# A hybrid encoder trunk: recurrence products issued in turns between halves of the array, and a bias for the decay's constant

## The chip, the cores and the metric

The kernel runs on one core of one Trainium2 chip. The metric is the device time of one execution in microseconds (us). Before the change three runs took 1224.38, 1223.29 and 1211.89 us; their median is 1223.29.

## What is computed

Two layers act on 256 tokens of 1024 channels, all in float32. Layer 0 mixes tokens with a bidirectional RWKV-7 recurrence, layer 1 with dilated attention. Behind each stands a mixture of 32 experts, of which every token uses two. Each part works on a normalised and modulated stream and adds to it; a last norm closes the trunk. The change lies in layer 0's mixer alone:

```python
def lora(xin, A, Bm, act):
    return jnp.einsum('zbsr,zre->zbse', act(jnp.einsum('bsd,zdr->zbsr', xin, A)), Bm)

w_log = -jax.nn.softplus(-(w0[:, None, None, :] + lora(xw, w1, w2, jnp.tanh))) - 0.5
decay = jnp.exp(-jnp.exp(w_log))
a = jax.nn.sigmoid(a0[:, None, None, :] + lora(xa, a1, a2, lambda t: t))
# per head of 64 channels and per direction z, step by step:
sa = jnp.einsum('bhvk,bhk->bhv', state, a_t)
state = state * w_t[:, :, None, :] + sa[..., None] * b_t[:, :, None, :] + v_t[..., None] * k_t[:, :, None, :]
y_t = jnp.einsum('bhvk,bhk->bhv', state, r_t)
```

## The kernel before, in words

The recurrence (`rwkv`) works on eight pairs of heads; a pair is 128 channels, so one head stands on partitions 0 to 63 and the other on 64 to 127. The 256 tokens are four chunks of 64. Both directions z run at once: at step s one is at chunk s, the other at chunk 3 - s. For each pair i:

- `project(i)` makes keys and receptances (`kr`), the decay's logarithm (`L`), the learning rate (`at`) and the values (`v`). `L` and `at` are second halves of LoRAs of rank 64 per direction. `L` has a 65th row: the hidden layer `hidw` ends in a row of ones and the weights in `w0`, so that the product adds it. `at` is added as a bias on ACT.
- `ready(i)` is `scale_keys(i)` and `chunks(i)`. `chunks` makes the chunk products `G`: for each direction and each head four products of 64 rows of the array by 128 columns into one PSUM bank, which DVE reads twice under masks (GV and GI).
- `inverse(i)` inverts the chunks' matrices by half-precision products (`iv`).
- `recur(i)` has for each of four steps: `R` (state times keys, not at step 0), `U` (inverse times R), `S` (the new states: an identity product carries the old one, two products add to it; not at step 3) and `Y` (the output: one product with the state, not at step 0, and two with `U`). `R` and `U` are issued in turns between the halves of the array already.
- `finish(i)` has the head norm, the bonus and the gate.

`weave` emits `recur(i)`, `inverse(i + 1)`, `finish(i - 1)`, `ready(i + 2)` and `project(i + 3)` side by side under priorities; a scheduler then sets the order of each engine's instructions. Every engine runs its own in that order, so an instruction that waits holds up all behind it. PSUM has eight banks: `pp` three (projections), `ps` two (`G`, `rn`, `sT`, `BT`, `R2`), `iv` two, `ch` one (`recur`).

A ring of 1 MB buffers takes the weights in the order of their use, and the queue SP issues each transfer when a buffer is free. The ring is two buffers long at first and grows as parts of the recurrence's memory are given back (`later`, behind pairs 4 to 7 and at the end). Line 266 is the helper of all matmuls, so they are told apart by their tiles. A float32 matmul appears in the trace as two passes.

Of the kernel before, what the change touches and what calls it, by code (L numbers as in the profile page):

```python
# [10 lines left out]
F32 = mybir.dt.float32  # L11
# [4 lines left out]
ALU = mybir.AluOpType  # L16
# [15 lines left out]
# share of the tensor engine's work of the streams that are woven, and their offset in priority  # L32
# [3 lines left out]
# eighths of the modulations that go with each pair of heads, and with each projection of the attention  # L36
ADA_PAIRS, ADA_PARTS = (0, 6, 6, 6, 8, 8, 8, 6, 0, 0, 0), (4, 4, 4, 4, 4, 4, 4, 4, 0)

# [1 line left out]
C_TMG, C_CMG, C_ADAB, C_C, C_FG = 0, 16, 32, 128, 136  # L40
N_COLS = 144
# (from here on for the recurrence only)
C_MU, C_KK, C_KA, C_RK, C_LNW, C_LNB, C_A0 = (N_COLS + n for n in (0, 48, 56, 64, 72, 80, 88))

# [1 line left out]
def _constants():  # L46
# [8 lines left out]
    # from here on for the recurrence only  # L55
# [34 lines left out]
def _half_constants():  # L90
    """identity, its negative, a 64 x 64 identity, the masks of the inverse's levels"""
    a, b = np.arange(64)[:, None], np.arange(64)[None, :]
    lv = np.zeros((64, 6, 64))
    for l in range(6):
        s = 1 << l
        lv[:, l] = ((a // (2 * s)) == (b // (2 * s))) & ((a // s) != (b // s))
    lv -= np.eye(64)[:, None]
    lv = lv.reshape(64, -1)
    e = np.tile(np.eye(64), (2, 1))
    return np.concatenate([np.eye(128), -np.eye(128), e, np.concatenate([lv, lv], 0),  # L100
                           np.kron(np.eye(2), lv[:, 0:64])], 1).astype(np.float16)
# [6 lines left out]
def _attn_constants():  # L108
    """Negative distances under the masks of the three groups; the tokens in the order even, odd."""
# [10 lines left out]
class Stream:  # L120
    """Blocks of weights, in the order in which they are used, through a ring of tiles.

    While a phase leaves room, a second pool lengthens the ring for the blocks before `limit`."""
# [38 lines left out]
    def spare(self):  # L162
        """A tile of the ring, once it holds all the blocks that are left."""
# [8 lines left out]
    def take(self, *names):  # L172
        """The next blocks; those taken before are used up."""
# [8 lines left out]
    def done(self):  # L182
        """The blocks taken last are used up."""
        for j in self.held:
            self.tiles.pop(j)
            self.owner.pop(j)[2] -= 1
        self.held = []
        self.fill()


# modulations (layer, kind, eighth) that are worked out before and during each token mixer
# [45 lines left out]
def trunk(ctx, tc, names, aps, out, stages=("rwkv", "moe0", "attn", "moe1"), dbg=None, ring=2):  # L237
# [16 lines left out]
    def banks(**n):  # L254
        """The banks of PSUM of a phase, by their uses."""
# [16 lines left out]
    def weave(*streams):  # L272
        """Emits streams side by side, each in step with its share of the tensor engine's work."""
# [87 lines left out]
    def ada_first(tag, acc):  # L361
        """Shift and scale of the first norm, by both engines."""
# [23 lines left out]
    def ada(i, m, k, tag="ps"):  # L386
        """An eighth of one of the six modulations."""
# [31 lines left out]
    def split(hi, lo, src, by, eng=None):  # L419
        """src times `by` (a power of two) as the sum of two numbers in half precision"""  # L420
# [12 lines left out]
    def scales(i, which):  # L433
        """columns of the modulated norm: scale, shift"""
# [8 lines left out]
    def new_sums(n=2):  # L443
        """the sums of squares of the tokens, in n parts of the channels"""
# [13 lines left out]
    def normalised(xn, tags):  # L458
        """the normalised stream in [d, t], two eighths of the channels in a bank each"""
# [17 lines left out]
    def transposed(j, behind=False):  # L477
        """a quarter of the stream's channels in [d, t]"""
# [9 lines left out]
    class Router:  # L488
        """Logits of the router, as the parts of x come in: its scale per token is put to the products."""
# [5 lines left out]
        def start(self):  # L495
            """The scaled weights, the part of the shift."""
# [14 lines left out]
        def hold(self, tag):  # L511
            """The bank and the sums that the parts of x go to."""
# [3 lines left out]
        def feed(self, t, c, junk):  # L516
            """a tile of tokens, half of the channels"""
# [23 lines left out]
    def gated(w, gate, k):  # L541
        """the rows of an output projection (k blocks side by side), times the gates of its columns"""
# [8 lines left out]
    def add_out(ps, t, c, by=1.0):  # L551
        """x += ps * by, in half of the channels of a tile of tokens"""
# [5 lines left out]
    def ada_share(n, tag="ps"):  # L558
        """The next n eighths of the modulations that go with layer 0."""
# [5 lines left out]
    def rwkv(pool):  # L565
        ctx2.enter_context(banks(pp=3, ps=2, iv=2, ch=1))
        cst_rw.append(pool.tile([128, 104], F32, name="colr"))
        nc.gpsimd.dma_start(out=cst_rw[0], in_=ap["p_colr"])
        sub = tc.alloc_tile_pool(name="sub", bufs=2, side="right", reuse_waits="tile")
        # (what the even pairs of heads use is given back before what the odd ones use)  # L570
# [5 lines left out]
        def pieces(tag):  # L576
            """tiles that are used before the recurrence needs their places"""
# [29 lines left out]
        # sigmoid(z) = 1/2 + tanh(z/2)/2, so that 1 + (a - 1) k_a = tanh k_a/2 + (1 - k_a/2)  # L607
        ka0, ka1 = (pool.tile([128, KD], F32, name=n) for n in ("ka0", "ka1"))
        a0h = pool.tile([128, 2 * KD], F32, name="a0h")
        # h, and half of both neighbours less h  # L610
# [3 lines left out]
        # (past the ends lies a zero, which the shift does not move)  # L614
# [32 lines left out]
        hidw = [sup.tile([65, S], F32, name=f"hidw{z}", bufs=1) for z in range(2)]  # L647
        hida = sup.tile([128, S], F32, name="hida", bufs=1)
        hidg = even.tile([128, 2, S], F32, name="hidg")

        def hidden():
            """LoRA hidden layers, [rank, t]"""
# [5 lines left out]
            for z in range(2):  # L658
                P.memset(hidw[z][64:65, :], 1.0)
                A.activation(out=hidw[z][0:64, :], in_=ps[64 * z:64 * z + 64, 0:S], func=AF.Tanh)  # L660
# [28 lines left out]
        # (two matrices of 64 x 64 each, on the diagonal)  # L689
# [18 lines left out]
        def both(t):  # L708
            """for both directions"""
            return t.unsqueeze(1).to_broadcast([128, 2] + list(t.shape[1:]))  # L710

        def project(i):
            """Projections of heads 2i and 2i + 1."""
# [9 lines left out]
            # 1 / max(|k k_k|, 1e-12) of each head, [t, (half of t, head)]  # L723
# [10 lines left out]
            w2 = vl[0:65, 1024:1280].rearrange("p (z n) -> p z n", z=2)  # L734
            a2 = vl[:, 1280:1408]
            ps = bank(name="L", tag="pp")
            L = sup.tile([128, 2, S], F32, name="L")
            for z in range(2):
                mm(ps[:, z * S:(z + 1) * S], w2[:, z, :], hidw[z])
            Lf = L.rearrange("p z t -> p (z t)")  # L740
            A.activation(out=Lf, in_=ps, func=AF.Tanh, scale=0.5)
            V.tensor_scalar(out=Lf, in0=Lf, scalar1=0.5 * DEC, scalar2=0.5 * DEC, op0=ALU.mult, op1=ALU.add)
            yield
            at = sup.tile([128, 2, S], F32, name="at")
            for z in range(2):
                ps = bank(name="at", tag="pp")
                mm(ps[:, 0:S], a2[half(z), :], hida[half(z), :])
                A.activation(out=at[:, z], in_=ps[:, 0:S], func=AF.Tanh,
                             scale=0.5, bias=a0h[:, 8 * z + i:8 * z + i + 1])
            w = ws[i] = dict(rn=rn, L=L, at=at, kT=krT[:, 0], rT=krT[:, 1])  # L750
            # values: channel-major, and token-major and centred by head
# [16 lines left out]
        def head_bcast(ps, v, n):  # L768
            """ps[channel, t] = v[t, head of the channel], for n blocks of 128 tokens"""
# [5 lines left out]
        def scale_keys(i, w):  # L775
            """Removal key, decays and the scaled operands, in [d, t]."""
            L, at, kT, rT = w["L"], w["at"], w["kT"], w["rT"]
            # sums of the logarithms over each chunk, in the directions' orders
# [4 lines left out]
            # running decays of each chunk, with a one before the first step: e1 up to a step, e3 up to the one before  # L783
# [30 lines left out]
            # bonus: (sum over the head) * v  # L814
# [4 lines left out]
            # (in use for three turns)  # L819
# [4 lines left out]
        def place(z, hh, c):  # L824
            """of a chunk's inverse: half of the partitions, number"""
            return half(1 - c % 2), (z * 2 + hh) * 2 + c // 2

        def chunks(i, w):
            """Chunk products, masked; token-major copies; the value part of the right-hand sides."""
# [4 lines left out]
            for z in range(2):  # L834
                for hh in range(2):
                    ps = bank(name="G")
                    for c in range(4):
                        mm(ps[:, c * 128:(c + 1) * 128], BK[half(hh), z, c, :], AR[half(hh), z, c, :])
                    for o, t in ((0, GV), (64, GI)):
# [5 lines left out]
            # the strictly triangular parts in two half-precision parts: half q holds chunk parity 1 - q  # L845
# [19 lines left out]
            # token rows of the recurrence: chunk parity p has its values on half p  # L865
# [16 lines left out]
        def inverse(i, w):  # L882
            """The chunks' (1 - A)^-1, transposed. By halves of ever larger blocks, in half precision; the residual
            is then taken with all of A's digits, and two terms of its series make up for it."""
# [15 lines left out]
            def parts(t):  # L900
                """The two blocks of the diagonal."""
                return [t[half(q), :, 64 * q:64 * q + 64] for q in range(2)]

            def spread(t, ps):
                """onto the diagonal, from PSUM"""
# [8 lines left out]
            # (Ah is A - 1 in half precision: A T - T has a diagonal of -1 and the blocks of A T below it)  # L914
# [48 lines left out]
        def recur(i, w):  # L963
            """The recurrence over chunks, both directions at once."""
# [3 lines left out]
            for s in range(4):  # L968
# [21 lines left out]
                if s < 3:  # L990
                    pS = bank(name="S", tag="ch")
                    for hh in range(2):
                        h, n = half(hh), slice(64 * hh, 64 * hh + 64)
# [958 lines left out]
```

## Time and profile before

| | before |
|---|---|
| median of three runs | 1223.29 us |
| the runs | 1224.38, 1223.29, 1211.89 us |
| span of the profiled execution (it has no other time) | 1225.3 us |
| PE busy | 1086.9 us (89%) |
| DVE busy | 660.5 us (54%) |
| ACT busy | 449.9 us (37%) |
| mean granted clock of TensorE | 0.936 |
| bytes moved | 322.46 MB, mean 263 GB/s |

Time is read from the stretch in which something happens, not from the shares over the whole span: the recurrence is the first 490 us or so, then come the experts of layer 0, the attention and the experts of layer 1. Matmuls are pipelined, so a group's cost is best read from its start to the start of the next group on PE, or over its first start to its last end.

### The profile page before, as it was taken

What the parts mean: (1) busy time and instruction counts of PE and PEld (TensorE: products, weight loads), DVE (VectorE), ACT (ScalarE), POOL (GpSimd) and SP (SyncE); (2) the same over time, 40 slices, a digit from 0 to 9 for tenths busy, and PEclk for the clock granted to TensorE, in tenths of its full rate; (3) what the DMA queues carried; (4) which work ended last, traced back from release to release, by engine and by line L of the source; (5) the groups of instructions that cost most, each with busy time, mean ns of one, the idle gap of its engine ahead of it and who ended that gap; (6) DMA issues with size and microseconds to landing.
All of it is one profiled execution on the core that took longest, in us unless ns stands there. A gap on an engine that the chain in (4) does not pass through costs nothing. (4 is left out here: it accounts for less than half of the span.)

```text
span 1225.3 us, 22879 instructions
## 1 busy us (share of the span) xinstructions
PE 1086.9 (89%) x9460; PEld 725.7 (59%) x9460; DVE 660.5 (54%) x1453; ACT 449.9 (37%) x940; POOL 177.8 (15%) x128
## 2 busy tenths in 40 slices
PE   4679999999999899897988879899988998799886
PEld 4556777777777664543443258778877864354432
DVE  8875477787774733522121166989986563122112
ACT  3326454464562552210010066546544531011002
POOL 6600001001120610000000012212283200000000
PEclk8789999999995999898998989989998999999989
DMA  9253164344352055898999996887653498989995
GB/s 373 101 206 117 35 204 125 123 156 133 106 173 103 2 241 221 333 422 352 422 421 421 420 419 240 315 319 290 237 197 138 168 361 358 417 366 421 421 420 229
DMA packets 53188, 322.46 MB, mean 263 GB/s; under 512 B 5922, under 2 KB 6562, under 8 KB 21458
## 3 DMA queue, kind: packets, MB, share of 16 engines
q1 hardware_dynamic: 51986, 316.49, 66.3%
q0 software_dynamic: 512, 2.30, 0.5%
q10 hardware_dynamic: 576, 2.10, 0.5%
q8 instruction: 78, 1.28, 0.4%
q14 instruction: 36, 0.29, 0.1%
HBM read 319.82 MB, written 1.05 MB: 262 GB/s over the span
## 5 line engine op out<-in xcount | busy, mean ns | idle before, releaser
L266 PE MATMUL gu<-wring,xT 128*32 128x512 f32 x1024 | 132.5, 619 | 16.9 <-DMA wring<-in_w_moe_dram 9.9
L358 DVE SCALAR_TENSOR_TENSOR acc<-aring,silu,acc 128x512 f32<-128x512 f32 x140 | 114.4, 849 | 9.5 <-DMA aring<-in_w_ada_dram 9.3
L425 POOL TENSOR_TENSOR wl<-wring,wh 128x1024 f16<-128x1024 f32 x24 | 57.2, 2383 | 407.1 <-DMA wring<-in_w_qkv_dram 241.0
L266 PE MATMUL qkv<-hl,wh 128*128 128x256 f16 x384 | 106.3, 277 | 2.0 <-DVE hl L1614 2.0
L266 PE MATMUL qkv<-hh,wl 128*128 128x256 f16 x384 | 106.4, 278 | 1.8 <-DVE wl L431 1.8
L266 PE MATMUL qkv<-hh,wh 128*128 128x256 f16 x384 | 106.6, 278 | 1.6 <-ACT hh L1613 1.6
L266 PEld LDWEIGHTS gu<-wring,xT 128*32 128x32 f32 x1024 | 31.8, 112 | 99.9 <-issue 80.4
L266 PEld LDWEIGHTS <-wh 128*128 128x128 f16 x768 | 76.4, 100 | 13.1 <-issue 3.6
L431 DVE SCALAR_TENSOR_TENSOR wl<-wring,wh 128x1024 f16<-128x1024 f32 x56 | 74.0, 1327 | 16.4 <-ACT wh L427 16.3
L266 PE MATMUL dn<-wring,hidT 128*32 128x256 f32 x1024 | 66.3, 407 | 18.1 <-ACT hidT L1416 18.0
L266 PE MATMUL acc<-y,back 128*128 128x512 f32 (+1 forms) x144 | 66.0, 581 | 10.3 <-DVE y L1443 8.1
L427 ACT ACTIVATE wh<-wring 128x1024 f16<-128x1024 f32 x56 | 58.6, 1050 | 35.4 <-PE qkv L266 30.8
L266 PEld LDWEIGHTS xT<-oh,x 128*128 128x128 f32 x512 | 59.0, 192 | 21.1 <-issue 9.2
L1218 DVE SCALAR_TENSOR_TENSOR sg<-sg,gu 128x256 f32<-128x256 f32 x16 | 6.7, 420 | 119.1 <-ACT sg L1217 119.1
L1443 DVE TENSOR_TENSOR y<-dn,ga 128x512 f32<-128x512 f32 x28 | 19.4, 692 | 88.9 <-PE dn L266 57.4
L266 PE MATMUL xT<-oh,x 128*128 128x128 f32 x512 | 63.5, 280 | 2.5 <-DVE oh L1327 2.5
L1217 ACT ACTIVATE sg<-gu 128x256 f32<-128x256 f32 x16 | 6.1, 383 | 153.1 <-PE gu L266 153.1
L266 PEld LDWEIGHTS dn<-wring,hidT 128*32 128x32 f32 x1024 | 32.1, 116 | 48.5 <-ACT hidT L1416 21.9
L1359 ACT ACTIVATE back<-bT 128x256 f32<-128x256 f32 x16 | 6.1, 384 | 131.7 <-PE acc L266 131.7
L266 PE MATMUL qkv<-wl,hh 128*128 128x256 f16 x192 | 54.0, 281 | 0.4 <-POOL wl L425 0.4
L266 PE MATMUL qkv<-wh,hl 128*128 128x256 f16 x192 | 53.9, 281 | 0.0
L266 PE MATMUL qkv<-wh,hh 128*128 128x256 f16 x192 | 53.9, 281 | 0.0
(341 smaller groups left out, 2292.0 us busy)
## 6 DMA issues: line engine op xcount, KB each, us to landing
wring<-in_w_moe_dram SPq DMA_DIRECT2D x192, 1024.0 KB, 19.8
aring<-in_w_ada_dram SPq DMA_DIRECT2D x96, 512.0 KB, 4.0
wring<-in_w_qkv_dram SPq DMA_DIRECT2D x36, 1024.0 KB, 8.5
wring<-in_w_kr_dram SPq DMA_DIRECT2D x8, 1024.0 KB, 5.1
wring<-in_w_vl_dram SPq DMA_DIRECT2D x8, 704.0 KB, 4.1
wring<-in_w_rwo_dram SPq DMA_DIRECT2D x4, 1024.0 KB, 5.9
wring<-in_w_ato_dram SPq DMA_DIRECT2D x4, 1024.0 KB, 6.5
ga<-in_p_adab_dram ACTq DMA_DIRECT2D x4, 512.0 KB, 3.8
```

The source lines that it names most:

```text
L266: return nc.tensor.matmul(out=o, lhsT=lhsT, rhs=rhs, start=start, stop=stop, **kw)
L358: V.scalar_tensor_tensor(out=acc[:, s], in0=w[:, s], scalar=silu[:, k:k + 1], in1=acc[:, s], op0=ALU.mult, op1=ALU.add)
L425: eng.tensor_tensor(out=lo, in0=src, in1=hi, op=ALU.subtract)
L427: A.activation(out=hi, in_=src, func=AF.Copy, scale=by)
L431: V.scalar_tensor_tensor(out=lo, in0=src, scalar=by, in1=hi, op0=ALU.mult, op1=ALU.subtract)
L1217: A.activation(out=o, in_=ps[:, 0:256], func=AF.Tanh, scale=0.5)
L1218: V.scalar_tensor_tensor(out=o, in0=o, scalar=1.0, in1=ps[:, 0:256], op0=ALU.add, op1=ALU.mult)
L1359: A.activation(out=back, in_=ps[:, 0:S], func=AF.Copy)
L1443: V.tensor_tensor(out=y, in0=py[c], in1=gates[i, 5][:, c * 512:(c + 1) * 512], op=ALU.mult)
```

## The change

In `chunks`, `G` opens two banks, one for each head, and issues the four chunks' products in turns between the heads, that is between the upper and the lower rows of the array. In `recur`, `S` issues the two identity products first, one for each half of rows and columns, and then the others in turns between the column halves; `Y` issues the two products with the state first and then the others in turns. The decay's LoRA loses its 65th row: `hidw` is one tile of 128 rows (rank 64 for both directions), the weights stand in 128 columns like those of `at`, `L` and `at` of one direction share a bank, and `w0` is added as a bias of the tanh (`w0h`, half of it, made once on DVE).

```diff
-        a0h = pool.tile([128, 2 * KD], F32, name="a0h")
+        a0h, w0h = (pool.tile([128, 2 * KD], F32, name=n) for n in ("a0h", "w0h"))
...
+        V.tensor_scalar(out=w0h, in0=col(C_W0, 2 * KD), scalar1=0.5, scalar2=None, op0=ALU.mult)
-        hidw = [sup.tile([65, S], F32, name=f"hidw{z}", bufs=1) for z in range(2)]
-        hida = sup.tile([128, S], F32, name="hida", bufs=1)
+        hidw, hida = (sup.tile([128, S], F32, name=n, bufs=1) for n in ("hidw", "hida"))
...
-            for z in range(2):
-                P.memset(hidw[z][64:65, :], 1.0)
-                A.activation(out=hidw[z][0:64, :], in_=ps[64 * z:64 * z + 64, 0:S], func=AF.Tanh)
+            A.activation(out=hidw, in_=ps[:, 0:S], func=AF.Tanh)
...
-            for z in range(2):
-                mm(ps[:, z * S:(z + 1) * S], w2[:, z, :], hidw[z])
+            pair = [bank(name="L", tag="pp") for _ in range(2)]
+            for n, hid in enumerate((hidw, hida)):
+                for z, ps in enumerate(pair):
+                    mm(ps[:, n * S:(n + 1) * S], vl[half(z), 1024 + 128 * n:1152 + 128 * n], hid[half(z), :])
+            for n, (t, b) in enumerate(((L, w0h), (at, a0h))):
+                for z, ps in enumerate(pair):
+                    A.activation(out=t[:, z], in_=ps[:, n * S:(n + 1) * S], func=AF.Tanh,
+                                 scale=0.5, bias=b[:, 8 * z + i:8 * z + i + 1])
             Lf = L.rearrange("p z t -> p (z t)")
-            A.activation(out=Lf, in_=ps, func=AF.Tanh, scale=0.5)
...
-            at = sup.tile([128, 2, S], F32, name="at")
-            for z in range(2):
-                ps = bank(name="at", tag="pp")
-                mm(ps[:, 0:S], a2[half(z), :], hida[half(z), :])
-                A.activation(out=at[:, z], in_=ps[:, 0:S], func=AF.Tanh,
-                             scale=0.5, bias=a0h[:, 8 * z + i:8 * z + i + 1])
...
             for z in range(2):
-                for hh in range(2):
-                    ps = bank(name="G")
-                    for c in range(4):
+                pair = [bank(name="G") for _ in range(2)]
+                for c in range(4):
+                    for hh, ps in enumerate(pair):
                         mm(ps[:, c * 128:(c + 1) * 128], BK[half(hh), z, c, :], AR[half(hh), z, c, :])
+                for hh, ps in enumerate(pair):
                     for o, t in ((0, GV), (64, GI)):
...
-                    for hh in range(2):
-                        h, n = half(hh), slice(64 * hh, 64 * hh + 64)
-                        if s > 0:
+                    hs = [(half(hh), slice(64 * hh, 64 * hh + 64)) for hh in range(2)]
+                    if s > 0:
+                        for h, n in hs:
                             mm(pS[h, 0:128], IDENT[h, n], ST[h, :, n], start=True, stop=False, skip_group_check=True)
-                        for z in range(2):
-                            c = cz[z]
+                    for z, c in enumerate(cz):
+                        for h, n in hs:
                             mm(pS[h, z * 64:z * 64 + 64], BT[:, c % 2, z, c // 2, n], UV[:, z, c, n],
...
-                for z in range(2):
-                    h = half(cz[z] % 2)
-                    if s > 0:
+                hs = [half(c % 2) for c in cz]
+                if s > 0:
+                    for z, h in enumerate(hs):
                         mm(py[h, 0:128], AR[:, z, cz[z], 64:128], ST[:, z, :], start=True, stop=False,
                            skip_group_check=True)
-                    for hh in range(2):
+                for hh in range(2):
+                    for z, h in enumerate(hs):
                         w["last"] = mm(py[h, hh * 64:hh * 64 + 64], GI[:, z, hh, cz[z], :], UV[:, z, cz[z], hh * 64:hh * 64 + 64],
...
-    vl = np.zeros((KD, 128, 1408), np.float32)
+    vl = np.zeros((KD, 128, 1280), np.float32)
```

The scheduler moves other instructions with them. On PE, pair 0's second step of the recurrence, with the chunk products of pair 1 (`G`), before:

```order
L266 MATMUL G_1071<-AR_1035,BK_1036 128x128
L266 MATMUL S_1351<-SD0_366,cst_67 64x128
L266 MATMUL S_1351<-UV_625,BT_612 64x64 x2
L266 MATMUL S_1351<-SD0_366,cst_67 64x128
L266 MATMUL S_1351<-UV_625,BT_612 64x64 x2
L266 MATMUL G_1071<-AR_1035,BK_1036 128x128 x3
L266 MATMUL G_1078<-AR_1035,BK_1036 128x128
L266 MATMUL Y_1383<-SD0_366,AR_490 64x128
L266 MATMUL Y_1383<-UV_625,GI_535 64x64 x2
L266 MATMUL Y_1383<-SD0_366,AR_490 64x128
L266 MATMUL Y_1383<-UV_625,GI_535 64x64 x2
```

The same place in the changed kernel (`kr` is a projection, `sT` the bonus):

```order
L266 MATMUL S_1349<-SD0_367,cst_67 64x128 x2
L266 MATMUL S_1349<-UV_623,BT_610 64x64 x4
L266 MATMUL sT_1048<-bb_1036,cstr_290 128x256 x2
L266 MATMUL Y_1381<-SD0_367,AR_488 64x128 x2
L266 MATMUL Y_1381<-UV_623,GI_533 64x64 x4
L266 MATMUL G_1055<-AR_1033,BK_1034 128x128 x2
L266 MATMUL G_1056<-AR_1033,BK_1034 128x128
L266 MATMUL R1_1434<-SD1_368,AR_488 64x128 x2
L266 MATMUL G_1056<-AR_1033,BK_1034 128x128
L266 MATMUL G_1055<-AR_1033,BK_1034 128x128
L266 MATMUL G_1056<-AR_1033,BK_1034 128x128
L266 MATMUL G_1055<-AR_1033,BK_1034 128x128
```

`S` and `Y` are in two rows each instead of four. `G`'s first two banks come later, and in turns only from their second product on, since the second bank is free later than the first. Over all pairs, eight of the sixteen `G` pairs still stand as four and four, and eight are in turns wholly or in part.

On DVE at the start of the program, before (`nss` and what follows is the first norm, `pUV` an accumulator of the modulations):

```order
L358 SCALAR_TENSOR_TENSOR pUV_195<-aring_80,silu_103,pUV_195 128x512 x2
L454 TENSOR_REDUCE nss_141<-sums_136 128x2
L455 TENSOR_SCALAR nss_141<-nss_141 128x2
L327 TENSOR_SCALAR rsy_144<-nss_141 128x2
L329 TENSOR_SCALAR rsh_145<-nss_141 128x2
```

And in the changed kernel:

```order
L358 SCALAR_TENSOR_TENSOR pUV_195<-aring_80,silu_103,pUV_195 128x512 x2
L454 TENSOR_REDUCE nss_141<-sums_136 128x2
L647 TENSOR_SCALAR w0h_304<-colr_123 128x16
L455 TENSOR_SCALAR nss_141<-nss_141 128x2
L327 TENSOR_SCALAR rsy_144<-nss_141 128x2
```

`w0h` needs the parameter columns (`colr`, a transfer of POOL's queue) and nothing else, so it stands as early as that. Behind the recurrence, the order of all engines' instructions is the same in both kernels.

## Rows read from the trace of the kernel before

**Rows 1.** The page: the span, and the rate of transfers in 40 equal slices.

```profile
span 1225.3 us, 22879 instructions
...
GB/s 373 101 206 117 35 204 125 123 156 133 106 173 103 2 241 221 333 422 352 422 421 421 420 419 240 315 319 290 237 197 138 168 361 358 417 366 421 421 420 229
```

**Rows 2.** Stretches: length, busy PE, PEld, DVE, ACT, POOL (instructions), clock, DMA share, GB/s.

```profile
120.00:200.00 80.00, 79.92 (x763) 60.21 (x762) 49.45 (x122) 38.31 (x86) 4.84 (x4) 0.98 0.35 117
200.00:300.00 100.00, 98.84 (x1076) 72.71 (x1074) 78.68 (x189) 54.18 (x116) 9.87 (x9) 0.98 0.43 137
...
582.00:735.00 153.00, 130.94 (x996) 62.64 (x995) 42.21 (x95) 31.08 (x69) 4.21 (x2) 0.96 1.01 421
```

**Rows 3.** PE's timeline, an S of a later step: start, length, what, shape, passes.

```profile
128.30 0.43 PE L266 MATMUL S<-SD,cst 64*64 64x128 f32 x2
128.66 0.45 PE L266 MATMUL S<-UV,BT 128*64 128x64 f32 x4
129.03 0.43 PE L266 MATMUL S<-SD,cst 64*64 64x128 f32 x2
129.39 0.45 PE L266 MATMUL S<-UV,BT 128*64 128x64 f32 x4
```

**Rows 4.** PE's timeline, S of a first step, then R and what follows it.

```profile
123.42 0.46 PE L266 MATMUL S<-UV,BT 128*64 128x64 f32 x8
...
126.12 0.44 PE L266 MATMUL R<-SD,AR 128*64 128x128 f32 x4
126.49 0.72 PE L266 MATMUL G<-AR,BK 64*128 64x128 f32 x6
```

**Rows 5.** PE's timeline, a Y of a later step.

```profile
130.63 0.43 PE L266 MATMUL Y<-SD,AR 128*64 128x128 f32 x2
...
130.90 0.32 PE L266 MATMUL Y<-SD,AR 128*64 128x128 f32 x1
...
131.07 0.50 PE L266 MATMUL Y<-UV,GI 128*64 128x64 f32 x5
```

**Rows 6.** PE's timeline, G of one half, then of two halves one behind the other.

```profile
84.76 1.16 PE L266 MATMUL G<-AR,BK 64*128 64x128 f32 x8
...
86.47 1.71 PE L266 MATMUL G<-AR,BK 64*128 64x128 f32 x16
```

**Rows 7.** The tile G: DVE's first read; duration in ns min/median/max, first and last start.

```profile
L840 DVE TENSOR_TENSOR GV<-G,cstr x32: 415/425/426, 85.9 to 426.2; 128x256 f32<-128x256 f32 x32
```

**Rows 8.** PE's timeline, L and at.

```profile
359.08 1.11 PE L266 MATMUL L<-hidw,wring 65*128 65x256 f32 x4
...
362.14 0.70 PE L266 MATMUL at<-hida,wring 64*128 64x256 f32 x4
```

**Rows 9.** Groups of ACT's instructions, 53 to 490 us: busy us, mean ns, idle before.

```profile
L748 ACT ACTIVATE at<-at,a0h 128x256 f32<-128x256 f32 x16 | 7.1, 472 | 3.7 <-PE at L266 3.5
...
L741 ACT ACTIVATE L<-L 128x512 f32<-128x512 f32 x8 | 4.8, 596 | 4.3 <-PE L L266 4.3
```

**Rows 10.** The tile colr: its transfer, a0h on DVE, and from issue to landing.

```profile
L568 POOL DMA_DIRECT2D colr<-in_p_colr_dram x1: 539/539/539, 3.1 to 3.1; - x1
...
L646 DVE TENSOR_SCALAR a0h<-colr x1: 161/161/161, 51.0 to 51.0; 128x16 f32<-128x16 f32 x1
...
DMA to landing us min/median/max: 8.5/8.5/8.5
```

**Rows 11.** DVE's timeline at the start.

```profile
11.95 0.15 DVE L454 TENSOR_REDUCE nss<-sums 128x2 f32<-128x4 f32 x1
```

**Rows 12.** Stretches around 370 us, columns as in rows 2.

```profile
365.00:370.00 5.00, 2.92 (x40) 2.24 (x40) 5.00 (x8) 1.91 (x5) 2.58 (x2) 0.98 0.00 0
370.00:400.00 30.00, 30.00 (x128) 22.91 (x128) 11.65 (x36) 8.13 (x18) 2.29 (x2) 0.50 0.27 106
```

**Rows 13.** PE's timeline before that; in brackets the idle time and what ended it.

```profile
369.92 2.07 PE L266 MATMUL sT<-bb,cstr 128*128 128x256 f32 x4 [2.05 <-DVE bb L815]
```

**Rows 14.** The tile Y: its products, first and last start.

```profile
L266 PE MATMUL Y<-UV,GI x256: 219/222/369, 124.9 to 487.1; 128*64 128x64 f32 x128
```

More of the change, by code (lines that the diff above doesn't have):

```diff
@@ L41 @@
 N_COLS = 144
-C_MU, C_KK, C_KA, C_RK, C_LNW, C_LNB, C_A0 = (N_COLS + n for n in (0, 48, 56, 64, 72, 80, 88))
+C_MU, C_KK, C_KA, C_RK, C_LNW, C_LNB, C_A0, C_W0 = (N_COLS + n for n in (0, 48, 56, 64, 72, 80, 88, 104))
 def _constants():
@@ L566, in rwkv @@
         ctx2.enter_context(banks(pp=3, ps=2, iv=2, ch=1))
-        cst_rw.append(pool.tile([128, 104], F32, name="colr"))
+        cst_rw.append(pool.tile([128, 120], F32, name="colr"))
         nc.gpsimd.dma_start(out=cst_rw[0], in_=ap["p_colr"])
@@ L733, in project @@
             vl = stream.take(("vl", i))
[L734 to L737, printed above, removed]
-            for z in range(2):
-                mm(ps[:, z * S:(z + 1) * S], w2[:, z, :], hidw[z])
+            L, at = (sup.tile([128, 2, S], F32, name=n) for n in ("L", "at"))
+            pair = [bank(name="L", tag="pp") for _ in range(2)]
[6 more added lines that the diff above has]
+                                 scale=0.5, bias=b[:, 8 * z + i:8 * z + i + 1])
             Lf = L.rearrange("p z t -> p (z t)")
-            A.activation(out=Lf, in_=ps, func=AF.Tanh, scale=0.5)
             V.tensor_scalar(out=Lf, in0=Lf, scalar1=0.5 * DEC, scalar2=0.5 * DEC, op0=ALU.mult, op1=ALU.add)
             yield
-            at = sup.tile([128, 2, S], F32, name="at")
-            for z in range(2):
-                ps = bank(name="at", tag="pp")
-                mm(ps[:, 0:S], a2[half(z), :], hida[half(z), :])
-                A.activation(out=at[:, z], in_=ps[:, 0:S], func=AF.Tanh,
-                             scale=0.5, bias=a0h[:, 8 * z + i:8 * z + i + 1])
             w = ws[i] = dict(rn=rn, L=L, at=at, kT=krT[:, 0], rT=krT[:, 1])
@@ L1895, in pack @@
         _cols(i["rw_mu"][0]), _cols(i["rw_k_k"][0]), _cols(i["rw_k_a"][0]), _cols(i["rw_r_k"][0]),
-        _cols(i["rw_ln_w"][0]), _cols(i["rw_ln_b"][0]), _cols(i["rw_a0"][0])], 1)
+        _cols(i["rw_ln_w"][0]), _cols(i["rw_ln_b"][0]), _cols(i["rw_a0"][0]), _cols(i["rw_w0"][0])], 1)
     o["w_ada"] = i["ada_w"].reshape(2, KD, 128, 6, D).transpose(0, 3, 1, 2, 4)
@@ L1909, in pack @@
     o["w_kr"] = np.concatenate([kr[1], kr[0]], 2)
-    vl = np.zeros((KD, 128, 1408), np.float32)
+    vl = np.zeros((KD, 128, 1280), np.float32)
     vl[:, :, 0:1024] = kr[2]
-    w2 = np.concatenate([i["rw_w2"][0], i["rw_w0"][0][:, None, :]], 1)
-    vl[:, 0:65, 1024:1280] = w2.reshape(2, 65, KD, 128).transpose(2, 1, 0, 3).reshape(KD, 65, 256)
-    vl[:, :, 1280:1408] = i["rw_a2"][0].reshape(128, KD, 128).transpose(1, 0, 2)
+    for n, w in enumerate(("rw_w2", "rw_a2")):
+        vl[:, :, 1024 + 128 * n:1152 + 128 * n] = i[w][0].reshape(128, KD, 128).transpose(1, 0, 2)
     o["w_vl"] = vl
```

## The prediction

> **What bounds the kernel now.** I read the page's slices first [rows 1]. A slice is 30.6 us. The recurrence layer fills the first sixteen; there the transfers run at 100 to 200 GB/s for the most part, and at 2 GB/s in the slice from 398 to 429 us: every buffer for weights is full, and the next ones are memory that the recurrence still holds. Then the table of stretches [rows 2]: from 120 to 200 us PE is busy for 79.92 of 80 us and from 200 to 300 us for 98.84 of 100, DVE for 49.45 and 78.68. From 582 to 735 us the transfers bound instead, at 421 GB/s. So PE's own row of instructions sets the recurrence's pace. What the recurrence gains, it gains for its memory too, so the stream of expert weights starts earlier by as much and all behind it moves along; the instructions behind the recurrence keep their order.
>
> Last, PE's timeline, for what one group of products takes from its start to the start of the next. Every float32 product stands there as two passes, so two products are a row with x4.
>
> **S, the state update.** For every step but the first, S is now one 64x64 product and two of 128x64 for one head, then the same for the other: four rows that last from 128.30 to 129.39 + 0.45 = 129.84 us, 1.54 us [rows 3]. The nearest rows for what replaces them: R, two products of the same 128 columns in turns between halves, four passes in 126.49 - 126.12 = 0.37 us; and the S of a first step, four 128x64 products on both halves, eight passes in 0.46 us [rows 4]. Two passes on one half alone take 128.66 - 128.30 = 0.36 us [rows 3], so the second half costs nothing. New: 0.37 + 0.46 = 0.83 us, 0.71 us less. There are 8 pairs of heads x 2 such steps = 16; all of it is 11.4 us. In the new order 12 of the 16 stand whole and other products cut into the other four; 12 x 0.71 = 8.5 is the low end. I take 10. A first step's S has the order changed too, but already takes the 0.46 us of a group in turns: nothing.
>
> The Trainium skill, "TensorE: Matmul & The Clock Gate", Part 3 (What overlaps and what doesn't), says that weight loads overlap running products only where the row groups differ, and R and S differ in columns alone. The trace disagrees: R's four passes took as long as two on one half. By the rule S and Y would win little; the case is a rival below.
>
> **Y, the output**, 3 steps x 8 = 24 groups of six products. Now 130.63 to 131.07 + 0.50 = 131.57, 0.94 us; the second half's first product (Y<-SD) starts 0.27 us in, ahead of passes that stand before it, so the array overlaps part already [rows 5]. New: R's 0.37 plus 0.46 = 0.83 us at most, as both parts have one shape; at least 0.94 - 0.27 = 0.67, the second half starting with the first. A gain of 0.11 to 0.27 each, 2.6 to 6.5 us; I take 0.2, 4.8 us.
>
> **G, the chunk products**, 16 pairs of groups. One half's four products take 1.16 us, both halves one behind the other 1.71 us [rows 6]; in turns both should take one half's time, as R does: 0.55 us less, 8.8 us in all. But both PSUM banks must then be free, and the new order shows that the scheduler still issues eight of the sixteen as four and four: eight remain, 8 x 0.55 = 4.4 us, which I take; some of them are in turns only for their second part, so 2.2 at the low end. What hides behind this: DVE reads each group twice at 0.425 us [rows 7], 1.70 us for a pair. Four groups with other work between them become two with a longer pause, which U, S, Y or projections fill in the order. Where they don't, PE waits.
>
> **L and at.** Four passes of L take 1.11 us, the four of `at` in turns between row halves 0.70 us [rows 8]; two groups like `at` are 1.40 against 1.81, 0.41 us x 8 = 3.3 us. At most both streams side by side last as long as L's four passes, 0.70 us less each, 5.6 us; at least nothing, where the order sets the four apart. I take 3.
>
> **Added.** ACT makes L's tanh in two pieces: 2 x 472 - 596 = 348 ns x 8 = 2.8 us, on an engine that is busy 54.18 of 100 us [rows 2, 9]: hidden by PE; all 2.8 us on the path if not. The one new DVE instruction scales `w0` (like a0h's 161 ns), and the scheduler puts it at the very start, behind the first reduction, where it waits for `colr`: issued at 3.1, landed 8.5 us later, 11.6, while DVE gets there at 11.95 + 0.15 [rows 10, 11]. So 0.2 us; queued behind it is the first norm. A transfer 1 us later than that costs 1 us. One tanh of `hidw` and two memsets less: at most 0.4 us. The value blocks are 64 KB smaller each, and the transfers' share there is 0.35 to 0.43 [rows 2]: nothing.
>
> **Sum.** 10 + 4.8 + 4.4 + 3 = 22.2 us of PE's time, bounds 8.5 + 2.6 + 2.2 + 0 = 13.3 and 11.4 + 6.5 + 8.8 + 5.6 = 32.3. Not all of it arrives: from 200 to 300 us DVE is at 79% [rows 2], and a stretch shorter by a sixteenth puts it at 84%, so some waits appear that were covered. I take four fifths, 18 us. The profiled execution has no time of its own beside its span of 1225.3 us [rows 1], which is 2.0 above the median of 1223.29 and 0.9 above the longest of the three runs: 1225.3 - 18 = 1207, and as a median **1205 us**.
>
> **The rivals.**
> - *Other engines take the place (0.22).* G's pairs wait for both banks and DVE becomes the bound. All sixteen pairs together need 16 x 1.70 = 27.2 us of DVE's reads. If G's 4.4 us vanish and half of the rest does, 9 us arrive: 1214. For it: DVE at 79%. Against: work stands between the pairs in the order. The Trainium skill, "TensorEngine Tiling (Array Packing)", PSUM Bottleneck, says the same: tiling speeds up the products, not the emptying of their banks; no row of before shows that as a loss.
> - *The clock (0.14, and the other side).* PE waited 2.05 us for DVE's bb before 369.92 us [rows 13], in a stretch where it was busy only 2.92 of 5 us; then the granted clock was 0.50, 1.2 GHz, from 370 to 400 us [rows 12]. G's passes there take twice as long, so a fall costs up to 30/2 = 15 us. Faster products mean more waits for DVE. With one more such fall, 1207 + 15 = 1222, no change (0.08); with two more, 1237, slower (0.06). It decides where PE stands still for some 2 us at a second and a third place of the recurrence; against it, 120 to 300 us has nearly no idle PE.
> - *The fall of before is gone (0.08).* The instructions around 368 us are in another order; without that wait 12 to 15 us more are won: about 1192. One of the three runs was at 1211.89, 11 below the median, with the same program.
> - *S and Y don't get what they were reordered for (0.04)*: weight loads for two column halves take turns, and R's 0.37 us has another reason. Then S and Y give between nothing and half of their 14.8 us, say 3, G and L their 7.4; four fifths of 10.4 is 8: 1215. This is the case of the rule above; R's row speaks against it.
>
> My forecast has 0.52. About 1% is what a measurement of this kernel can tell from no change: below 1211 is faster, above 1235.5 slower. Faster: forecast 0.52 + lost fall 0.08 = 0.60. Same: 0.22 + 0.08 + 0.04 = 0.34. Slower: 0.06. The range: at the low end all of 22.2 us arrives and most of the cost of one clock fall goes, 1223 - 22 - 12 = 1189; at the high end one more fall, 1222.
>
> **What would show it.** S, steps two and three: the four rows become one SD row of x4 and one UV row of x8, 0.83 us. Y: 0.67 to 0.83 us. G in turns: 16 passes in about 1.2 us. L: eight passes in 1.1 to 1.4 us. The last Y, which starts at 487.1 us [rows 14], starts near 469, the 421 GB/s stretch starts as much earlier, the end follows. Wrong if groups shorten but idle PE before G or sT grows (the first rival), if the stretch at 0.50 is longer or comes twice, or if each group takes what it took.

## The result and the profile after

| | before | after |
|---|---|---|
| median | 1218.76 us (20 runs) | 1204.02 us (20 runs) |
| range | 1204.15 to 1224.66 us | 1195.12 to 1208.52 us |
| ratio of the runs compared | | 0.991, 95% interval [0.988, 0.9939] |
| profiled execution, span | 1225.3 us | 1196.7 us |
| PE, DVE, ACT busy | 1086.9, 660.5, 449.9 us | 1058.2, 662.4, 452.1 us |
| mean granted clock | 0.936 | 0.941 |

The kernel became faster by 0.6 to 1.2%, 11 us by the ratio and 14.7 us by the medians. The ratio shows less because it leaves out runs more than 1.5% above the fastest of their kernel, here six of the kernel before (above 1222.2 us) and none of the changed one. The profiled executions differ by more, 28.6 us of span: the one of before is among the longest of its kernel and the one of after, with a time of 1199.71 us, lies 4.3 us below its median.

The table of stretches of the changed kernel (columns as in [rows 2]), with the span from its page:

```profile
span 1196.7 us, 22898 instructions
...
120.00:200.00 80.00, 79.41 (x838) 58.27 (x839) 54.24 (x137) 41.75 (x91) 5.97 (x5) 1.00 0.39 130
200.00:300.00 100.00, 99.36 (x1143) 72.23 (x1142) 80.29 (x193) 60.74 (x133) 10.17 (x10) 1.00 0.47 155
...
553.00:711.00 158.00, 137.22 (x1055) 64.95 (x1056) 42.53 (x97) 30.99 (x71) 4.21 (x2) 0.92 1.01 419
```

PE is as full as before in the first two, and does 838 passes in place of 763 and 1143 in place of 1076. DVE rises only to 80 us of 100: PE still sets the pace. The stretch at 420 GB/s is there again, some 24 to 29 us earlier.

PE's timeline of the changed kernel around pair 0's second step (start, us, then engine, line, operation, tiles, shape, count); it answers to [rows 3 to 6]:

```profile
123.65 0.44 PE L266 MATMUL S<-SD,cst 64*64 64x128 f32 x4
124.01 0.45 PE L266 MATMUL S<-UV,BT 128*64 128x64 f32 x8
124.39 1.13 PE L266 MATMUL sT<-bb,cstr 128*128 128x256 f32 x4
125.45 0.44 PE L266 MATMUL Y<-SD,AR 128*64 128x128 f32 x4
125.72 0.40 PE L266 MATMUL Y<-UV,GI 128*64 128x64 f32 x8
126.05 0.81 PE L266 MATMUL G<-AR,BK 64*128 64x128 f32 x6
...
130.21 0.72 PE L266 MATMUL G<-AR,BK 64*128 64x128 f32 x8
...
165.68 0.70 PE L266 MATMUL L<-hidw,wring 64*128 64x256 f32 x4
166.21 0.60 PE L266 MATMUL L<-hida,wring 64*128 64x256 f32 x4
...
252.79 0.70 PE L266 MATMUL L<-hidw,wring 64*128 64x256 f32 x4
253.43 0.41 PE L266 MATMUL iv<-X,TTd 128*128 128x64 f16 x8
253.76 0.70 PE L266 MATMUL L<-hida,wring 64*128 64x256 f32 x4
```

S takes 124.46 - 123.65 = 0.81 us (1.54 before), Y 126.12 - 125.45 = 0.67 us (0.94). Eight passes of G on both halves take 0.72 us; on one half they took 1.16. L's eight passes take 1.13 us where they stand together, at 165.68, and 0.70 twice where the scheduler puts `iv` between them, as at 252.79. The tile Y's products show what it adds up to [rows 14]:

```profile
L266 PE MATMUL Y<-UV,GI x256: 219/222/315, 119.3 to 463.6; 128*64 128x64 f32 x128
```

The last Y starts at 463.6 us, 23.5 earlier. Added up over the trace from each pass's start to the next pass's, from 53 us to the last Y:

| PE's time on | before | after | change | taken in the forecast |
|---|---|---|---|---|
| S | 28.4 | 18.4 | -10.0 | -10 |
| Y | 29.3 | 23.4 | -5.9 | -4.8 |
| G | 40.3 | 35.4 | -4.9 | -4.4 |
| L and at | 18.5 | 17.0 | -1.5 | -3 |

The sum is 22.2 us (from unrounded times). In the same stretch the clock was at 0.50 for 52.4 us before and for 39.5 us after (time at 0.50 is counted from 53 us to the last Y here and below). About half of the difference, 6.5 of the 23.5 us, is the clock's. This is an estimate: half of the time at 0.50 is taken as lost, since the passes of `kr` follow each other after 0.427 us there and after 0.216 us at 1.00 (medians in the kernel before). By the same count, without the clock, S takes 8.6 us less, Y 5.8, G 5.5 and L with at 2.1, some 22 us in all.

PE's stretches from 53 us to the last Y, of the kernel before and of the changed one:

```profile
53.00:487.08 434.08, 413.90 (x4126) 300.86 (x4125) 279.10 (x659) 210.17 (x450) 66.00 (x59) 0.94 0.40 138
53.00:463.58 410.58, 386.22 (x4125) 276.56 (x4124) 279.70 (x659) 211.96 (x457) 67.59 (x59) 0.95 0.41 145
```

PE is idle for 434.08 - 413.90 = 20.2 us of the first and for 410.58 - 386.22 = 24.4 us of the second: the waits grew by 4.2 us.

The long fall of before [rows 12, 13] has a shorter successor. Stretches of the changed kernel:

```profile
345.00:352.00 7.00, 4.18 (x48) 2.69 (x43) 6.96 (x10) 5.29 (x14) 5.05 (x4) 1.00 0.18 73
352.00:363.00 11.00, 10.68 (x42) 7.52 (x42) 7.59 (x22) 2.34 (x4) 1.39 (x1) 0.53 0.00 1
```

And what stands in front of it, by the timelines of DVE, POOL and PE of the changed kernel, and last by those of POOL and DVE of the kernel before:

```profile
346.75 0.15 DVE L336 SCALAR_TENSOR_TENSOR rsy<-rsq,rsy 128x4 f32<-128x4 f32 x1
...
348.83 1.76 DVE L358 SCALAR_TENSOR_TENSOR acc<-aring,silu,acc 128x512 f32<-128x512 f32 x1
350.51 1.75 DVE L810 SCALAR_TENSOR_TENSOR bb<-krT,colr,kd 128x512 f32<-128x512 f32 x1
...
346.95 6.44 POOL L548 TENSOR_TENSOR wring<-wring,ga 128x512 f32<-128x512 f32 x4 [7.60 <-DMA wring<-in_w_rwo_dram]
...
352.32 1.14 PE L266 MATMUL sT<-bb,cstr 128*128 128x256 f32 x2 [2.84 <-DVE bb L810]
...
362.28 5.30 POOL L548 TENSOR_TENSOR wring<-wring,ga 128x512 f32<-128x512 f32 x4 [5.37 <-PE Y L266]
...
362.43 1.24 DVE L334 TENSOR_TENSOR rsq<-rsy 128x4 f32<-128x4 f32 x1
```

While POOL multiplies (346.95 to 353.39), DVE's L810 takes 1.75 us, where 0.74 is usual; PE waits 2.84 us for it, and then the clock is at half for 10 us. This collision is older than the change: in the kernel before, POOL's same products (362.28 to 367.58) stand ahead of the wait of 2.05 us for bb at 369.92 [rows 13], and a DVE operation that takes 0.15 us elsewhere takes 1.24.

### The profile page after: what moved, and what is told of

Same layout as the page of the kernel before. It is cut to its first block, busy times and chain, and to the rows that moved or that the text cites. A ratio compares the mean times of both kernels' runs of the same rounds, so it can differ in the third digit from the quotient of the medians.

```text
span 1196.7 us, 22898 instructions
## 1 busy us (share of the span) xinstructions
PE 1058.2 (88%) x9460; PEld 700.4 (59%) x9460; DVE 662.4 (55%) x1454; ACT 452.1 (38%) x947; POOL 175.5 (15%) x126
```

## The experiments

Each ratio is to the kernel before on the same chip (medians 1222.04, 1224.14 and 1221.68 us on three chips).

**One part at a time.** S alone, Y alone, G alone, and the LoRA part alone, each being the change's own lines on the kernel before. Of S:

```diff
-                    for hh in range(2):
-                        h, n = half(hh), slice(64 * hh, 64 * hh + 64)
-                        if s > 0:
+                    hs = [(half(hh), slice(64 * hh, 64 * hh + 64)) for hh in range(2)]
+                    if s > 0:
+                        for h, n in hs:
...
```

S: 

> S alone is issued in turns (state update), everything else as before. Theory A (the array's time adds up, four fifths arrive): S loses 0.71 us in each of 16 later steps, 10 us on PE, 8 us of the end: ratio 0.993; in the trace S<-SD x4 then S<-UV x8, 0.83 us from first start to last end. Theory B (the gain is the recurrence's chain: S and Y stand in it, G and L do not): 8 us or a little more, since the next step's R waits for S. Theory C (the difference between the two profiles is mostly granted clock): no ratio outside 0.995 to 1.005.

Y: 

> Y alone is issued in turns. Theory A: 0.27 us less in each of 24 later groups (0.94 to 0.67 us), 6.5 us on PE, 5 us of the end: ratio 0.996. Theory B: Y ends a step and nothing of the next step waits for it, so PE's 6.5 us at most. Theory C: no difference.

G: 

> G alone gets two banks and turns. Theory A: 4.4 us on PE, 3.5 us of the end: ratio 0.997. Theory B (banks): the pair holds both banks of its tag, rn, sT, BT and R2 wait for them, PE's idle time before G and sT grows by as much: ratio 1.000 to 1.004.

LoRA: 

> The decay's LoRA alone is changed (bias instead of the 65th row, L and at in turns over row halves in two shared banks). Theory A: 3 us on PE, 2.4 us of the end: ratio 0.998. Theory B (banks): L's two banks are held until at is done, yT, kr and v of the same tag wait: ratio 1.000 to 1.003.

| part | median | ratio, interval | its own time on PE | last Y | at 0.50 before it |
|---|---|---|---|---|---|
| none (before) | 1222.04 | | | 487.1 | 52.4 |
| S | 1217.09 | 0.997 [0.9933, 1.0007] | 28.4 to 19.6 | 478.7 | 47.8 |
| Y | 1216.67 | 0.9976 [0.9932, 1.002] | 29.3 to 23.5 | 481.8 | 51.2 |
| G | 1216.91 | 0.9971 [0.9932, 1.001] | 40.3 to 33.5 | 476.2 | 35.1 |
| LoRA | 1223.51 | 1.0051 [1.0015, 1.0088] | 18.46 to 17.54 | 486.8 | 51.2 |

S, Y and G each shorten their own groups and the recurrence; the medians are 5.0, 5.4 and 5.1 us lower. Each interval alone still includes 1, so none of the three alone excludes theory C, that the difference is mostly the clock's; the next run, with all three, does. The last Y by itself flatters G: with half of the time at 0.50 taken off, it comes 6.1 us earlier by S, 4.7 by Y and 2.3 by G (estimates). The LoRA part alone brings nothing: 0.9 us less of products, the last Y where it was, and by its ratio it is 0.2 to 0.9% slower. Its trace does not show where that is lost.

**The change without the LoRA part.** All of the change's lines but those of `w0h`, `hidw`, `pair` for L and the table of weights.

> S, Y and G in turns, the LoRA part left as before. Theory (the LoRA part costs more elsewhere than the 1 us it saves in products): the three gains of 5.0, 5.3 and 5.1 us add, 0.986 to 0.988 of the kernel before, some 1206 us against 1222, that is 3 to 6 us below the changed kernel's 0.991; last Y near 464 us. Rival (the LoRA part earns its 3 us, and the 0.5% by which it was slower alone is a matter of one schedule): 0.993 to 0.994, last Y near 466 to 468 us.

1206.75 us, ratio 0.9856 [0.9778, 0.9935]: the three gains add (15.5 us by the parts, 17.4 by the medians). But its last Y is at 470.1 us, 6.5 later than with the LoRA part, and its interval covers the changed kernel's 0.991. So the theory that the LoRA part costs fell in one view and held in the other. Most of the 6.5 us is the clock's: 49.5 us were at 0.50 here against 39.5, 5 us by half; the 1.5 us left are no more than what L and at gained on PE in the changed kernel. The pair of runs with and without it, below, settles it more closely.

**G held in turns.** In the changed kernel the scheduler still issues eight of sixteen pairs as four and four:

```diff
-                        mm(ps[:, c * 128:(c + 1) * 128], BK[half(hh), z, c, :], AR[half(hh), z, c, :])
+                        with tc.issue_after(turn.ins) if c or hh else nullcontext():
+                            turn = mm(ps[:, c * 128:(c + 1) * 128], BK[half(hh), z, c, :], AR[half(hh), z, c, :])
```

> The changed kernel with the products of G held strictly in turns between the halves for all sixteen pairs (by an order that the scheduler must keep). Theory of the sum (each pair that is still issued as four and four loses 0.55 us): 8 x 0.55 = 4.4 us less of PE's time, some 3.5 arrive, ratio 0.988, last Y near 460 us. Rival (both banks must be free at once, and DVE's two reads of 0.425 us of each end later): PE waits before G, G's share of idle time grows by 4 us or more, no gain or up to 4 us slower than the changed kernel, ratio 0.991 to 0.995.

1195.44 us, ratio 0.9812 [0.9748, 0.9877], better than either theory, and the last Y is at 452.3 us. G's time fell from 35.4 to 27.8 us, or from 30.5 to 27.2 with half of its time at 0.50 taken off: 3.3 us where the theory had 4.4. PE's timeline and stretches of this kernel:

```profile
125.29 0.71 PE L266 MATMUL G<-AR,BK 64*128 64x128 f32 x6
126.01 0.44 PE L266 MATMUL S<-SD,cst 64*64 64x128 f32 x4
...
351.69 0.41 PE L266 MATMUL iv<-X,Td 128*128 128x64 f16 x8 [2.21 <-DVE Td L944]
...
345.00:352.00 7.00, 3.94 (x53) 2.57 (x50) 6.96 (x13) 5.01 (x11) 6.13 (x4) 1.00 0.24 98
352.00:365.00 13.00, 12.89 (x124) 9.46 (x122) 10.33 (x33) 6.19 (x14) 1.27 (x2) 0.99 0.41 151
```

The groups are still cut, into twos, sixes and fourteens for the most part, but always in turns. The feared wait for two banks came once, with 0.5 us; the one long wait before G in the recurrence is the 2.27 us for DVE's AR that the changed kernel has too. In this trace the last Y comes 11.3 us earlier, and the clock alone explains that: 17.1 us were at 0.50, 22.4 less than in the changed kernel, and half of that is 11.2. What G saves is taken back elsewhere (PE is idle for 26.2 us in place of 24.4, and other groups take longer). Why the clock falls less here is open. PE waits 2.21 us at 351.69 here, is busy 3.94 of 7 us, and the clock does not fall.

**The collision taken away.** POOL's gating of the output projection's weights (L548) is held until its last operand of the seventh pair, in the kernel before and in the changed one:

```diff
-                w = gated(stream.take(("rwo", 0, c)), gates[0, 2][:, c * 512:(c + 1) * 512], 4)
+                with tc.issue_after(ws[6]["al"].ins):
+                    w = gated(stream.take(("rwo", 0, c)), gates[0, 2][:, c * 512:(c + 1) * 512], 4)
...
```

The lines left out give that last operand the name `al` and hold the second half of the weights back in the same way.

In the kernel before: 

> The kernel before, but POOL multiplies the first output-projection blocks by their gates only after its last operand of the seventh pair of heads, not while DVE works on the running sums of the fourth; nothing else is changed. Theory of the clock (the stretch of 30.7 us at 0.50 from 369.8 us starts because PE stood still 2.05 us for DVE's bb): DVE's small operations there take 0.15 in place of 1.24 us, the wait before sT falls under 1 us, the stretch at 0.50 goes or comes elsewhere and shorter, last Y some 12 to 15 us earlier (472 to 475 us), ratio 0.988 to 0.991. Rival (the clock falls for another reason than that wait): the wait is gone, low clock in all stays 45 to 55 us, last Y 484 to 488 us, ratio 0.997 to 1.002.

In the changed kernel: 

> The changed kernel with POOL's gating held back in the same way. Theory of the clock: the wait of 2.84 us before sT at 352.3 us goes, and with it the 10.2 us at 0.50 that follow it: 2.8 + 5 us less at most, last Y 456 to 459 us, ratio 0.985 to 0.987. Rival: the wait goes and the low clock stays at 35 to 45 us in all: last Y 461 to 464 us, ratio 0.989 to 0.992.

The kernel before with it: 1213.63 us, ratio 0.9949 [0.9913, 0.9984], last Y at 472.0. DVE, PE and the stretch after, in its trace:

```profile
359.71 0.16 DVE L336 SCALAR_TENSOR_TENSOR rsy<-rsq,rsy 128x4 f32<-128x4 f32 x1
...
361.38 0.75 DVE L815 SCALAR_TENSOR_TENSOR bb<-krT,colr,kd 128x512 f32<-128x512 f32 x1
...
362.59 1.13 PE L266 MATMUL sT<-bb,cstr 128*128 128x256 f32 x4
...
362.00:374.00 12.00, 11.78 (x89) 8.84 (x90) 8.44 (x28) 4.63 (x12) 0.00 (x0) 1.00 0.35 130
```

The wait before sT is gone, the clock stays at 1.00 until a fall of 6.8 us at 374.5, and time at 0.50 falls from 52.4 to 27.3 us: 12.5 us by half of it and 2 by the wait, and the last Y comes 15.1 us earlier. The theory holds on the place and on this trace; over the runs the gain is 6 us by the ratio, 10.5 by the medians, less than the 0.988 to 0.991 that the theory had. The changed kernel with it: 1196.07 us, ratio 0.9821 [0.9757, 0.9884], last Y 454.8 us, 20.5 us at 0.50. Its stretches:

```profile
352.00:363.00 11.00, 10.98 (x104) 8.64 (x106) 7.33 (x28) 4.18 (x11) 2.57 (x3) 1.00 0.63 235
363.00:370.00 7.00, 5.01 (x84) 3.59 (x81) 5.47 (x6) 3.55 (x9) 7.00 (x5) 1.00 0.20 83
```

**The collision put where there was none.** On the kernel before, at the fifth pair:

```diff
+            if i == 4:
+                scr = sup.tile([128, S], F32, name="scr", bufs=1)
+                for _ in range(10):
+                    P.tensor_tensor(out=scr, in0=kk, in1=kk, op=ALU.mult)
```

> The kernel before, with ten POOL products of 128x256 on a scratch tile added at the fifth pair of heads, beside DVE's small operations ahead of the sT near 272 us, where the clock was 1.00; nothing reads their result. Theory (DVE is slowed beside POOL's products, PE then waits for bb, and a wait of 2 us or more brings a stretch at 0.50): DVE's operations of 0.15 us take over 1 us, PE waits 2 to 4 us before that sT, and 10 us or more at 0.50 follow within 5 us of it: last Y 7 to 15 us later. Rival (a wait alone does not bring the clock down): the wait costs itself, 2 to 4 us, and the granted clock from 270 to 300 us stays 1.00.

1228.72 us, median of 9 (1207.40 to 1234.56), against 1221.68 of 14 (1209.20 to 1233.21): the ranges overlap, and nothing is concluded from these times, only from the trace. POOL, DVE, PE and the stretches of this kernel, and last the same two stretches of the kernel before:

```profile
261.89 8.89 POOL L800 TENSOR_TENSOR scr<-kk 128x256 f32<-128x256 f32 x10 [3.70 <-DVE rsy L327]
...
264.13 0.57 DVE L332 SCALAR_TENSOR_TENSOR rsq<-rsq 128x4 f32<-128x4 f32 x1
...
264.95 0.57 DVE L333 SCALAR_TENSOR_TENSOR rsy<-rsq,rsy 128x4 f32<-128x4 f32 x1
...
270.29 0.41 PE L266 MATMUL iv<-X,Td 128*128 128x64 f16 x8 [1.23 <-DVE Td L951]
...
271.38 1.56 PE L266 MATMUL sT<-bb,cstr 128*128 128x256 f32 x4 [0.45 <-DVE bb L819]
...
378.25 1.13 PE L266 MATMUL sT<-bb,cstr 128*128 128x256 f32 x4 [2.05 <-DVE bb L819]
...
265.00:280.00 15.00, 13.07 (x87) 9.79 (x85) 12.36 (x29) 6.42 (x14) 5.31 (x7) 0.73 0.11 36
280.00:300.00 20.00, 20.00 (x102) 13.24 (x101) 9.40 (x26) 4.46 (x12) 2.30 (x2) 0.69 0.32 92
...
378.00:390.00 12.00, 11.75 (x83) 8.70 (x84) 8.75 (x29) 4.59 (x12) 0.00 (x0) 1.00 0.40 140
...
265.00:280.00 15.00, 14.70 (x157) 11.12 (x157) 13.13 (x39) 10.33 (x24) 0.00 (x0) 1.00 0.37 134
280.00:300.00 20.00, 20.00 (x186) 13.83 (x184) 15.22 (x33) 7.78 (x17) 2.65 (x3) 1.00 0.40 124
```

DVE's small operations took 0.57 us in place of 0.15, PE stood still 1.23 and 0.45 us at 269 to 271, less than the theory asked for, and from 272 us the clock was at 0.50 for 20.5 us, in a place where it had been at 1.00. So in this one execution the delay of PE was followed by a fall that the same place did not have before. But the old wait, 2.05 us for the same bb, still stands before 378.25, and this time the clock stayed at 1.00 for the next 13 us. In all 50.1 us were at 0.50, and the last Y was at 485.8, near the 487.1 of before: the expected shift of 7 to 15 us did not come, since one stretch took the other's place.

**All together, with and without the LoRA part, and with L held in turns.** The edits are those above; the last has the same `issue_after` on L's four products:

```diff
+                    with tc.issue_after(turn.ins) if n or z else nullcontext():
+                        turn = mm(ps[:, n * S:(n + 1) * S], vl[half(z), 1024 + 128 * n:1152 + 128 * n], hid[half(z), :])
```

With it: 

> The changed kernel with G held strictly in turns and POOL's gating held back, both. Theory (both took away much of the same low clock, 39.5 us falling to 17.1 and to 20.5, so the gains don't add in full): ratio 0.976 to 0.980, last Y 446 to 450 us, low clock before it under 20 us. Rival (they add): 0.991 - 0.010 - 0.009 = 0.972, last Y near 443 us.

Without it: 

> The same without the LoRA part. Theory (the LoRA part saves some 2 us of products and its later tanh takes them back): within 0.3% of the kernel with it, last Y within 3 us. Rival 1 (it costs 0.5%, as alone): 0.5% lower than the kernel with it. Rival 2 (it earns its 3 us and more, as the last Y of 470.1 against 463.6 us in the profiles without and with it says): last Y 3 us or more later than with it, ratio 0.2 to 0.5% higher.

L in turns: 

> The version with everything, and L's four products of a pair held in turns too, so that all eight passes stand as one group of 1.06 us in place of two of 0.63. Theory: at most 8 x 0.2 = 1.6 us of PE's time, ratio lower by 0.1% or nothing. Rival (the group must wait for two free banks of the three that the projections use): idle PE before L, the same or up to 3 us slower.

| version | median | ratio, interval | last Y | at 0.50 before it | span |
|---|---|---|---|---|---|
| all | 1194.37 | 0.9804 [0.9762, 0.9846] | 451.4 | 17.1 | 1185.2 |
| all, no LoRA part | 1194.33 | 0.9794 [0.9758, 0.983] | 455.6 | 23.9 | 1190.7 |
| all, L in turns | 1185.98 | 0.9737 [0.969, 0.9784] | 450.2 | 17.1 | 1183.0 |

Holding G in turns and holding POOL back don't add: each alone had left 17.1 and 20.5 us at 0.50 of 39.5, and both together leave 17.1. With and without the LoRA part the times are equal, so it is worth nothing that these runs can tell, to within some 0.5%. L held in turns is the best version of all, 2.6% below the kernel before and clearly below the changed one. Why it is 0.7% below the version next to it is open: the scheduler cut L's group as before (whole, 1.06 us, in one pair of the eight in both), PE's time on L was 18.8 and 18.0 us, the last Y differs by 1.2 us, and the two intervals overlap.

## Why the prediction was right

The cause that it named is the one that the runs show: S, Y and G take less of PE's time in turns, PE sets the pace, and most of it arrives. In its own terms:

- **S, 10 us:** right. 0.81 us a step for the 0.83 forecast, and 10.0 us in all (8.6 without the clock). The prediction says that S differs in columns alone; that holds for its products with UV, while the identity products differ in rows too (64*64 [rows 3]). The rival by which weight loads for two column halves take turns is refuted: eight passes on both halves take as long as four on one.
- **Y, 4.8 us:** 5.9. A whole group takes 0.67 us, the bound that was set by the second half starting with the first, and not the 0.74 that I took between the bounds.
- **G, 4.4 us:** 4.9. The condition was seen rightly from the order, that half of the pairs would not be in turns. Holding them took another 7.6 us off G's time, more than half of it through the clock (3.3 us without it).
- **L and at, 3 us:** the term that was mis-sized, in an otherwise right sum. 1.5 us in the changed kernel, 0.9 alone. For seven pairs it is nearly what was priced (13.7 to 11.3 us against 7 x 0.41 = 2.9). The first pair loses 0.9 us, 5.68 for 4.77. PE's timeline there, of the kernel before and then of the changed one:

```profile
61.29 1.11 PE L266 MATMUL L<-hidw,wring 65*128 65x256 f32 x4
65.43 0.70 PE L266 MATMUL at<-hida,wring 64*128 64x256 f32 x4 [3.03 <-DVE kss L730]
...
61.40 0.70 PE L266 MATMUL L<-hidw,wring 64*128 64x256 f32 x2
65.37 0.49 PE L266 MATMUL L<-hidw,wring 64*128 64x256 f32 x1 [3.28 <-DVE kss L729]
...
65.70 1.44 PE L266 MATMUL L<-hida,wring 64*128 64x256 f32 x3
```

  PE waits until DVE has read the sums `ss` and so given a bank back. Before, L's four passes ran ahead of that wait and only `at` stood behind it; now L and `at` share banks, two passes run ahead and six stand behind. The clock falls to 0.50 there in both kernels, at 66.06 us before, behind the last pass of `at`, and at 65.72 us after, so that most of the six run at half: some 0.7 of the 0.9 us is that (an estimate, half of 65.72 to 67.07 us), the rest the longer wait. The forecast had neither the wait nor the clock at this place.
- **Four fifths arrive, 18 us:** right in the trace once the clock is taken out, a little too much over many runs. The last Y moved by 23.5 us; without the 6.5 us of the clock it moved by 17.0, of 22.2 on PE, and PE's idle time grew by 4.2 us, as the forecast had it. The end moved by 28.6; but the medians moved by 14.7 us and the ratio says 11. That 1205 met 1204.02 so closely is partly luck: the three runs with their median of 1223.29 stood 4.5 us above the median of twenty, so the forecast time was met with a gain smaller than the one forecast.
- **Added work:** right at nothing. `w0h` ran at 12.01 us, right behind the first reduction at 11.95, without a wait for its transfer.
- **The clock:** the rival's price, 12 to 15 us for the long stretch, is what the last Y gained (15.1 us) when the collision was taken away. Its condition, that PE stands still for some 2 us, does not decide by itself. In seven traces (before, changed, S, Y, G, LoRA, and the change without the LoRA part) PE waits 2.05 to 3.68 us for bb before this sT, and a stretch of 10 to 31 us at 0.50 begins within 2 us of the wait. But the same wait of 2.05 us was followed by none in the next 12 us in the kernel with POOL's added products, 2.21 us by none with G in turns, and 1.23 + 0.45 us by 20.5 us. And a short fall can come where PE did not wait at all, as in the kernel before:

```profile
184.00:192.00 8.00, 8.00 (x64) 6.51 (x60) 6.00 (x13) 1.77 (x4) 2.30 (x2) 1.00 0.38 123
192.50:195.50 3.00, 3.00 (x16) 1.86 (x14) 1.05 (x2) 1.46 (x4) 0.00 (x0) 0.50 0.57 175
```

  What else it takes is open.

## What to carry to other kernels

Products that use half of the array, on rows or on columns, took 0.53 (S) to 0.71 (Y) of the time here when they alternated between the halves: write that order and then look whether the scheduler keeps it; where it doesn't, try holding it. Where an engine's small delay (here POOL against DVE) makes the array wait, price the low clock that may follow (here 10 to 31 us at half behind waits of 2 to 4 us), and judge a change by many runs and by the place where its stage ends, with the time at low clock counted beside it, not by two profiled spans.

## What was not expected of the hardware

- DVE's operations with two inputs wait until the POOL product that is running has ended: 0.57 us in place of 0.15 beside POOL products of 128x256 (ten in 8.89 us), each delayed one ending within 0.02 us of a POOL product's end, and 1.24 beside those of 128x512 (four in 5.30 us, from 362.28 us in the kernel before). The Trainium skill, "SBUF — State Buffer", Who interferes with whom, says that the two share a port pair and that the later one "fully blocks" until the earlier is done; the trace agrees.
- In the kernel before, the clock stayed at 0.50 for 30 us while PE was busy for 30.00 of 30.00 us [rows 12]. The Trainium skill, "TensorE: Matmul & The Clock Gate", Part 1 (The HAM clock gate), has the clock come back once the array is busy again; here, beside shorter stretches, it did so only after 10 to 31 us in the seven stretches behind the wait for bb.
- The spread between runs of one program is the clock's too: of 66 runs of the kernel before, the shortest, 1208.17 us, had a mean granted clock of 0.961, the longest, 1235.41 us, one of 0.936. A straight line through the 66 gives 6.3 us of span for 0.01 of the mean clock (correlation -0.82). Against this line, at equal clock, the twenty runs of the changed kernel lie 17.9 us lower, S, Y and G alone 6 us each, and the LoRA part alone 2.5 us higher (estimates; the changed kernel's twenty runs were not taken beside these 66).
